# The FFN up projection: fourteen of 22 pairs take their seven products in a row, with other buffers

## The chip, the cores and the metric

The kernel runs on one core of a Trainium2 chip. Its engines have queues of their own: TensorE (PE; its weight loads are PEld), VectorE (DVE), ScalarE (ACT), GpSimd (POOL) and SyncE (SP), which issues every DMA here. Each queue runs in order, and engines wait for each other by semaphores. The metric is the time of one execution in microseconds (us) on the device; lower is better.

## The reference

One decoder layer on 1024 positions of 1024 channels in float32: a convolution branch and a state-space branch are mixed, then comes a ConvFFN. Only the ConvFFN's first half is touched:

```python
def conv_ffn(h, w_up, dw_w, dw_b, w_down):
    u = causal_dwconv(h @ w_up, dw_w, dw_b)        # w_up: 1024 x 5632, three taps
    gate, val = jnp.split(u, 2, axis=-1)           # 2816 channels each
    return (jax.nn.silu(gate) * val) @ w_down
```

## The kernel before

A float32 product is made of three matmuls of a rounded type: each operand is split into a high part (a ScalarE copy with rounding) and a low part (a VectorE subtraction), and `mm3` (lines 162 to 167) adds high x high, high x low and low x high into one bank. All matmuls of the ConvFFN thus carry lines 165 to 167, and all weight splits lines 153/154 (`weights`) or 730/731 (`split_pair`).

The up projection `h @ w_up` multiplies by Winograd's variant of Strassen's scheme: seven block products where eight would stand. A *pair* is one 128-channel block of the gate and one of the values. 22 pairs (`NF`) are made. The activations' blocks `b11`, `b21`, `b22` and sums `t1` to `t4` are prepared by `ffn_blocks`, which also holds the layer norm before it. A `product` (line 715) is four steps in depth, 12 matmuls of 128x512, into one of eight banks: four of the tag `acc` (`bank(1)`), four of the tag `sm` (`bank(0)`).

For pair j two products need the raw weights alone. `up_first` (line 805) loads them into `st_ue`, splits them as `w_ue`, makes w11 x b11, copies the result out (`s`, line 811), adds w21 x b21 into the same bank, and copies again (`c`, line 815). Both results go to `first_scr` in DRAM. The other five are made by `up_rest` (line 837). Its `up_weights` (line 818) loads both raw tiles of the pair again (`ra`, `rb`), makes sums of their halves in place on VectorE (lines 828 to 831), and splits three tiles: `w_s24`, `w_s10` and `w_s3` (lines 730/731, all named `w_s` in the trace; the sum of w3 is `s3`, shown as `s`). `s` and half of `ug` come back from `first_scr` (lines 846, 847). Three `sm` banks take five products (t2; t1; t3; b22 on top of t1's bank; t4 on top of t3's), and five VectorE instructions (lines 853 to 861) add or subtract them into `s`, `ug` and `uv` (`fug`, `fuv` in the trace). The convolution then takes one ScalarE scaling and two VectorE taps for each of the two blocks (lines 867, 871), ScalarE's silu (881) and the gating (882). Every second pair adds four block sums (896 to 899) and stores results for the down projection.

Order: eight firsts (`LEAD`) run ahead, while `ffn_blocks` ends; the 14 others are spread over the 22 calls of `up_rest`. Instructions are placed by a scheduler that plays the program through with planned times and takes what is ready by priority; `tc.high_priority(offset=...)` pulls loads and splits ahead. Each queue's order is then fixed. A pool lends buffers by tag: `wst` has three raw buffers (`st`), `wsp` three of split weights (`w`), `up` three of raw pair weights (`raw`). A tile waits until the earlier tile in its buffer is released. Pools that follow each other share memory: `up` takes that of `trans` (used by `ffn_blocks`), and `down` that of `ffq`.

The down projection (line 903) begins with eight `rows` loads (line 920), which need the buffer of the blocks b11 and b21, and its steps load `dr` raw tiles (952, 954), `c` tiles (955, 959) and split them (990, 991, `w_dn`). The tiles `c4` lie where `ffq` held b22, t1 and t2.

Of the kernel before, what the change touches and what calls it, by code (L numbers as in the profile page):

```python
# [21 lines left out]
FF = 2816  # L22
NF = FF // P
KC = 31
HEADS = 32
GROUPS = 4
HP = 64
# [28 lines left out]
def kernel(  # L56
# [30 lines left out]
    def bank(which):  # L87
        n_ps[0] += 1
        pl, tag = (pacc, "acc") if which else (psm, "sm")
        return pl.tile([P, 512], F32, tag=tag, name=f"{tag}{n_ps[0]}")  # L90
# [44 lines left out]

    h_scr = [dram.tile([HALF, D], F32, name=f"h_scr{i}") for i in range(2)]
    h1_scr = dram.tile([T, D], F32, name="h1_scr")
    first_scr = [dram.tile([2, P, HALF], F32, name=f"first_scr{j}") for j in range(NF)]
    NK = NF // 2
    b11_scr = [dram.tile([P, HALF], F32, name=f"b11_scr{k}") for k in range(NK)]  # L140
    b2_scr, t32_scr, t41_scr = (
# [660 lines left out]
            "t4": lambda i: b2[0][:, i, 4:8, :],  # L802
        }

    def up_first(qp, bl, j):

        w = weights(wup[2 * j], f"ue{j}")
        ps = bank(1)
        product(ps, lambda i: w[:, i, 0:HALF], bl["b11"], True)
        s1 = qp.tile([P, HALF], F32, tag="first", bufs=2, name=f"s1_{j}")  # L810
        A.copy(s1, ps)  # L811
        SY.dma_start(first_scr[j][0], s1)
        product(ps, lambda i: w[:, i, HALF:D], bl["b21"], False)
        c11 = qp.tile([P, HALF], F32, tag="first", bufs=2, name=f"c11_{j}")
        A.copy(c11, ps)
        SY.dma_start(first_scr[j][1], c11)

    def up_weights(upp, j):


        with tc.high_priority(offset=2000):
            r1 = upp.tile([P, D], F32, tag="raw", bufs=3, name=f"ra{j}")
            SY.dma_start(r1, wup[2 * j])
            r2 = upp.tile([P, D], F32, tag="raw", bufs=3, name=f"rb{j}")
            SY.dma_start(r2, wup[2 * j + 1])
            a11, a12, a21, a22 = r1[:, :HALF], r1[:, HALF:], r2[:, :HALF], r2[:, HALF:]
            s3 = upp.tile([P, HALF], F32, tag="s3", name=f"s3_{j}")
            V.tensor_tensor(out=s3, in0=a11, in1=a21, op=ALU.add)
            V.tensor_tensor(out=a21, in0=a21, in1=a22, op=ALU.add)
            V.tensor_tensor(out=a11, in0=a21, in1=a11, op=ALU.add)  # L830
            V.tensor_tensor(out=a12, in0=a12, in1=a11, op=ALU.add)
            w24 = split_pair(wsp, r1, f"s24_{j}")
            w10 = split_pair(wsp, r2, f"s10_{j}")
            w3 = split_pair(upp, s3, f"s3_{j}", HALF, 2)
        return w24, w10, w3

    def up_rest(upp, bl, j, before):

        w24, w10, w3 = up_weights(upp, j)
        ug, uv = (
            upp.tile([P, T + 32], F32, tag="u", bufs=3, name=f"f{n}{j}") for n in ("ug", "uv")
        )
        s = upp.tile([P, HALF], F32, tag="s", bufs=2, name=f"s{j}")
        SY.dma_start(s, first_scr[j][0])
        SY.dma_start(ug[:, 2 : 2 + HALF], first_scr[j][1])
        G.memset(ug[:, :2], 0.0)
        G.memset(uv[:, :2], 0.0)
        pb, pc_, pd = bank(0), bank(0), bank(0)  # L850
        late = slice(2 + HALF, 2 + T)
        product(pb, lambda i: w24[:, i, :HALF], bl["t2"], True)
        V.tensor_tensor(out=s, in0=s, in1=pb, op=ALU.add)
        product(pd, lambda i: w10[:, i, :HALF], bl["t1"], True)
        V.tensor_tensor(out=uv[:, late], in0=s, in1=pd, op=ALU.add)  # L855
        product(pc_, lambda i: w3[:, i], bl["t3"], True)
        V.tensor_tensor(out=uv[:, late], in0=pc_, in1=uv[:, late], op=ALU.subtract)
        product(pd, lambda i: w24[:, i, HALF:], bl["b22"], False)
        V.tensor_tensor(out=ug[:, late], in0=s, in1=pd, op=ALU.add)
        product(pc_, lambda i: w10[:, i, HALF:], bl["t4"], False)  # L860
        V.tensor_tensor(out=uv[:, 2 : 2 + HALF], in0=pc_, in1=s, op=ALU.subtract)
        os = []
        j = j // 2 + j % 2 * NK
        for jj, u in ((j, ug), (NF + j, uv)):
            o = upp.tile([P, T], F32, tag="o", bufs=3, name=f"fo{jj}")
            wc = PC_FW + 3 * jj
            A.activation(
                out=o, in_=u[:, 2 : 2 + T], func=AF.Identity, scale=pc[:, wc + 2 : wc + 3]
            )
            for k in range(2):  # L870
                V.scalar_tensor_tensor(  # L871
                    out=o,
                    in0=u[:, k : k + T],
                    scalar=pc[:, wc + k : wc + k + 1],
                    in1=o,
                    op0=ALU.mult,
                    op1=ALU.add,
                )
            os.append(o)
        og, ov = os  # L880
        A.activation(out=og, in_=og, func=AF.Silu, bias=pc[:, PC_FB + j : PC_FB + j + 1])
        V.scalar_tensor_tensor(
            out=ov,
            in0=ov,
            scalar=pc[:, PC_FB + NF + j : PC_FB + NF + j + 1],
            in1=og,
            op0=ALU.add,
            op1=ALU.mult,
        )
        early, late = slice(0, HALF), slice(HALF, T)  # L890
        if j < NK:
            SY.dma_start(b11_scr[j], ov[:, early])
            return ov
        SY.dma_start(b2_scr[j - NK], ov)
        a, b, t = before, ov, og
        V.tensor_tensor(out=t[:, early], in0=a[:, late], in1=b[:, late], op=ALU.subtract)
        V.tensor_tensor(out=a[:, late], in0=a[:, early], in1=a[:, late], op=ALU.subtract)
        V.tensor_tensor(out=t[:, late], in0=t[:, early], in1=a[:, early], op=ALU.subtract)
        V.tensor_tensor(out=a[:, early], in0=b[:, early], in1=t[:, late], op=ALU.add)
        SY.dma_start(t32_scr[j - NK], t)  # L900
        SY.dma_start(t41_scr[j - NK], a)

    def down(upp, dp, g, b):
# [32 lines left out]
        def load(p, k):  # L936
# [12 lines left out]
            with tc.high_priority(offset=4000):  # L949
                st = raw("dr")  # L950
                w_st = st[:, E]
                SY.dma_start(st[:, L], x)
                if p == 0:
                    SY.dma_start(w_st, a11)
                    SY.dma_start(c3[k], a21)
                    add(c3[k], c3[k], w_st)
                elif p == 1:
                    SY.dma_start(w_st, a12)
                    SY.dma_start(c4[k], a22)
                    add(c4[k], c4[k], w_st)  # L960
                elif p == 2:
                    SY.dma_start(w_st, a22)
                    add(w_st, w_st, c3[k])
                elif p == 3:
                    w_st = c3[k]
                    add(c4[k], c4[k], c3[k])
                elif p == 4:
                    other = raw("do")[:, E]
                    SY.dma_start(w_st, a21)
                    SY.dma_start(other, a22)  # L970
                    add(w_st, w_st, other)
                elif p == 5:
                    SY.dma_start(w_st, a22)
                else:
                    w_st = c4[k]
                if p == 6 and k >= NK - 4:
                    if not last:
                        last.append(big_tile("last").rearrange("p i k t -> p (i k t)"))
                    w = last[0][:, (k - NK + 4) * 2 * D : (k - NK + 5) * 2 * D]
                    w = w.rearrange("p (i n) -> p i n", i=2)  # L980
                else:
                    own = n_steps % 2 and n_steps > 4
                    w = (dp if own else wsp).tile(
                        [P, 2, D], F32R, tag="w", bufs=3, name=f"w_dn{p}_{k}"
                    )
                cuts = ((slice(0, D), st),) if w_st is not c3[k] and w_st is not c4[k] else (
                    (E, w_st), (L, st[:, L])
                )
                for cs, src in cuts:
                    A.copy(w[:, 0, cs], src)  # L990
                    V.tensor_tensor(  # L991
                        out=w[:, 1, cs], in0=src, in1=w[:, 0, cs].bitcast(F32), op=ALU.subtract
                    )
# [89 lines left out]
    qp = ffn_stack.enter_context(pool("ffq", side="right"))  # L1083
    with pool("trans") as tp:
        bl = ffn_blocks(tp, qp, mixT)
    n_first = 0

    def firsts_to(n):
        nonlocal n_first
        while n_first < min(n, NF):  # L1090
            up_first(qp, bl, n_first)
            n_first += 1

    LEAD = 8
    firsts_to(LEAD)
    upp = ctx.enter_context(pool("up"))
    before = None
    for j in range(NF):
        firsts_to(LEAD + (j + 1) * (NF - LEAD) // (NF - 1))
        before = up_rest(upp, bl, j, before)  # L1100
    ffn_stack.close()
    dp = ctx.enter_context(pool("down", side="right"))
# [101 lines left out]
```

## Time and profile before

| | us |
|---|---|
| median of three runs | 2030.39 (2029.87 to 2030.8) |
| profiled execution, its own time | 2030.96 |
| span of that execution | 2029.3 |
| first and last start of a `w_ue` matmul | 1356.0, 1767.4 |

The profile is of one execution. Times in rows are microseconds from the span's start, or of one instruction; names in a row are output <- inputs, without buffer numbers, so `acc<-h1b,w_ue` is a first product, `sm<-h1s,w_s` and `sm<-h1b,w_s` are the products of `up_rest`, and `acc<-w_dn` belongs to the down projection. A bracket behind a row gives how long the engine sat idle before it and what ended that. `SPq` rows are DMA issues. A matmul's duration overlaps the next one's; the distance of starts is the rate.

### The profile page before, as it was taken

To read this page: it belongs to the slowest core of one execution; us is meant where nothing else is said; L and a number is where in the kernel's file an instruction comes from. 1 tells how busy PE (TensorE), PEld (TensorE's weight loads), DVE (VectorE), ACT (ScalarE), POOL (GpSimd) and SP (SyncE) were. 2 spreads that over 40 slices of the span, in tenths; PEclk is the share of its full clock that TensorE was granted. 3 is DMA by queue.
4 is the path that set the end of the run, shared out by engine and by line. 5 is a ranking of instruction groups with operands and counts; after the bars stand their busy time and mean duration, and the time that the engine had idled before them with its cause. 6 is when DMAs were issued, how large, how long until landed. Compare 5 with 4: busy or idle time off the path is not lost. (4 is left out here: it accounts for less than half of the span.)

```text
span 2029.3 us, 24897 instructions
## 1 busy us (share of the span) xinstructions
PE 1973.4 (97%) x9164; PEld 1624.7 (80%) x9164; DVE 1732.8 (85%) x2307; ACT 987.5 (49%) x1403; POOL 147.1 (7%) x125
## 2 busy tenths in 40 slices
PE   7999999999999999999999999999999999989998
PEld 6888887888788888888888888887878788768886
DVE  7599999989766868999998976586899899889768
ACT  4465654556453265665454635364444344334432
POOL 2010101001400000100100121001000000000000
PEclk9999999999999999999999999999999999999999
DMA  6222233332545532222323254576545545578463
GB/s 219 94 64 93 80 102 106 98 105 99 166 126 194 214 104 73 89 83 84 115 89 117 96 171 129 169 252 223 166 161 199 169 161 197 184 292 279 161 226 109
DMA packets 109274, 297.14 MB, mean 146 GB/s; under 512 B 12384, under 2 KB 12384, under 8 KB 109152
## 3 DMA queue, kind: packets, MB, share of 16 engines
q1 hardware_dynamic: 109152, 295.55, 43.7%
q8 instruction: 72, 1.18, 0.2%
q14 instruction: 50, 0.41, 0.1%
HBM read 238.61 MB, written 56.89 MB: 146 GB/s over the span
## 5 line engine op out<-in xcount | busy, mean ns | idle before, releaser
L419 DVE SCALAR_TENSOR_TENSOR c<-v,pc,c 128x512 f32<-128x512 f32 x480 | 374.9, 804 | 8.4 <-ACT c L408 7.0
L477 POOL TENSOR_TENSOR au<-seg_mv,head_of 128x1024 fp32r<-128x1024 f32 x32 | 76.9, 2403 | 963.6 <-PE sm L486 730.1
L165 PE MATMUL acc<-hT,w_c 128*128 128x512 f32 x352 | 141.0, 401 | 0.0
L166 PE MATMUL acc<-hT,w_c 128*128 128x512 f32 x352 | 140.5, 399 | 0.0
L167 PE MATMUL acc<-hT,w_c 128*128 128x512 f32 x352 | 138.4, 393 | 0.0
L165 PE MATMUL sm<-h1s,w_s 128*128 128x512 f32 x264 | 104.6, 396 | 11.2 <-DVE fuv L855 9.1
L374 DVE SCALAR_TENSOR_TENSOR xbc<-u,pc,xbc 128x512 f32<-128x512 f32 x144 | 109.8, 775 | 0.7 <-ACT xbc L372 0.5
L990 ACT CAST w_dn<-dr 128x1024 fp32r<-128x1024 f32 (+1 forms) x73 | 68.7, 945 | 83.7 <-DVE dr L924 32.4
L166 PE MATMUL sm<-h1s,w_s 128*128 128x512 f32 x264 | 103.5, 392 | 0.0
L167 PE MATMUL sm<-h1s,w_s 128*128 128x512 f32 x264 | 102.8, 392 | 0.0
L166 PE MATMUL acc<-w_z,hT 128*128 128x512 f32 x256 | 100.8, 394 | 0.0
L165 PE MATMUL acc<-w_z,hT 128*128 128x512 f32 x256 | 100.8, 401 | 0.0
L167 PE MATMUL acc<-w_z,hT 128*128 128x512 f32 x256 | 100.7, 396 | 0.0
L153 ACT CAST w_c<-st_c 128x1024 fp32r<-128x1024 f32 x50 | 52.5, 1051 | 86.4 <-PE acc L167 65.6
L991 DVE TENSOR_TENSOR w_dn<-dr,w_dn 128x1024 fp32r<-128x1024 f32 (+1 forms) x73 | 78.9, 1089 | 11.2 <-ACT w_dn L990 11.1
L166 PEld LDWEIGHTS acc<-hT,w_c 128*128 128x128 f32 x352 | 66.1, 188 | 16.9 <-issue 3.8
L167 PEld LDWEIGHTS acc<-hT,w_c 128*128 128x128 f32 x352 | 66.1, 188 | 16.1 <-issue 2.6
L165 PEld LDWEIGHTS acc<-hT,w_c 128*128 128x128 f32 x352 | 66.1, 188 | 15.9 <-issue 2.6
L154 DVE TENSOR_TENSOR w_c<-st_c,w_c 128x1024 fp32r<-128x1024 f32 x47 | 60.6, 1289 | 20.3 <-ACT w_c L153 20.3
L165 PE MATMUL acc<-h1b,w_ue 128*128 128x512 f32 x176 | 70.0, 398 | 6.8 <-ACT s L811 6.8
L165 PEld LDWEIGHTS sm<-h1s,w_s 128*128 128x128 f32 x264 | 50.1, 190 | 25.9 <-DVE fuv L855 12.2
L166 PE MATMUL acc<-h1b,w_ue 128*128 128x512 f32 x176 | 69.5, 395 | 0.0
(336 smaller groups left out, 5723.1 us busy)
## 6 DMA issues: line engine op xcount, KB each, us to landing
st_c<-wcol SPq DMA_DIRECT2D x50, 512.0 KB, 3.6
st_z<-wz SPq DMA_DIRECT2D x32, 512.0 KB, 3.5
dr<-wdown SPq DMA_DIRECT2D x55, 256.0 KB, 4.5
st_wo<-wo SPq DMA_DIRECT2D x24, 512.0 KB, 4.0
st_ue<-wup SPq DMA_DIRECT2D x22, 512.0 KB, 3.8
ra<-wup SPq DMA_DIRECT2D x22, 512.0 KB, 3.6
rb<-wup SPq DMA_DIRECT2D x22, 512.0 KB, 3.9
t_scr<-fo SPq DMA_DIRECT2D x22, 512.0 KB, 3.5
```

The source lines that it names most:

```text
L153: A.copy(w[:, 0, :], st)
L154: (eng or V).tensor_tensor(out=w[:, 1, :], in0=st, in1=w[:, 0, :].bitcast(F32), op=ALU.subtract)
L165: TE.matmul(ps, wa(0), xa(0), start=start, stop=False, skip_group_check=more)
L166: TE.matmul(ps, wa(0), xa(1), start=False, stop=False, skip_group_check=more)
L167: TE.matmul(ps, wa(1), xa(0), start=False, stop=stop, skip_group_check=more)
L374: V.scalar_tensor_tensor(out=o, in0=u[:, k : k + HALF], scalar=pc[:, wc + k : wc + k + 1], in1=o, op0=ALU.mult, op1=ALU.add,)
L419: V.scalar_tensor_tensor(out=accs[i], in0=v[:, k : k + HALF], scalar=pc[:, wc + k : wc + k + 1], in1=accs[i], op0=ALU.mult, op1=ALU.add,)
L477: G.tensor_tensor(out=au, in0=seg_mv[:, c, :].unsqueeze(1).to_broadcast([P, 8, P]), in1=head_of[:, g, :].unsqueeze(2).to_broadcast([P, 8, P]),
L990: A.copy(w[:, 0, cs], src)
L991: V.tensor_tensor(out=w[:, 1, cs], in0=src, in1=w[:, 0, cs].bitcast(F32), op=ALU.subtract)
```

## The change

The firsts of pairs 0 to 7 run ahead as before, with a pool of their own (`firsts`, four buffers), which is closed before the pool `up` is opened. The 14 other pairs have no first any more: their seven products are made by `up_rest`, from one load of each raw tile. A third split, `w_ue`, is taken from `ra` before the sums overwrite it, in the pool `wsp`. Two `acc` banks are used (`ps`, `py`): b11, t2, t1 and b22 accumulate in `ps`, and ScalarE copies the bank out after each of them into `s`, `s`, `uv` and `ug`; b21 goes to `py`, which VectorE adds to `s`. VectorE thus has three evictions in such a pair in place of five. In all pairs t3 now comes before t1, and t4 before b22.

The raw tile `ra` moves to the pool `wst` (three buffers), and `rb` has the three of `up` to itself. In the down projection the split tiles use the pool `dp` from step 3 on, in place of step 5.

```diff
-    def up_first(qp, bl, j):
+    def up_first(fp, bl, j):
...
-        product(ps, lambda i: w[:, i, 0:HALF], bl["b11"], True)
-        s1 = qp.tile([P, HALF], F32, tag="first", bufs=2, name=f"s1_{j}")
-        A.copy(s1, ps)
-        SY.dma_start(first_scr[j][0], s1)
-        product(ps, lambda i: w[:, i, HALF:D], bl["b21"], False)
-        c11 = qp.tile([P, HALF], F32, tag="first", bufs=2, name=f"c11_{j}")
-        A.copy(c11, ps)
-        SY.dma_start(first_scr[j][1], c11)
+        for q, block in enumerate(("b11", "b21")):
+            product(ps, lambda i: w[:, i, q * HALF : (q + 1) * HALF], bl[block], q == 0)
+            f = fp.tile([P, HALF], F32, tag="first", bufs=4, name=f"first{q}_{j}")
+            A.copy(f, ps)
+            SY.dma_start(first_scr[j][q], f)
...
-            r1 = upp.tile([P, D], F32, tag="raw", bufs=3, name=f"ra{j}")
+            r1 = wst.tile([P, D], F32, tag="st", name=f"ra{j}")
...
+            ue = None if j < LEAD else split_pair(wsp, r1, f"ue{j}")
...
-        SY.dma_start(s, first_scr[j][0])
-        SY.dma_start(ug[:, 2 : 2 + HALF], first_scr[j][1])
...
-        pb, pc_, pd = bank(0), bank(0), bank(0)
-        late = slice(2 + HALF, 2 + T)
-        product(pb, lambda i: w24[:, i, :HALF], bl["t2"], True)
-        V.tensor_tensor(out=s, in0=s, in1=pb, op=ALU.add)
-        product(pd, lambda i: w10[:, i, :HALF], bl["t1"], True)
-        V.tensor_tensor(out=uv[:, late], in0=s, in1=pd, op=ALU.add)
-        product(pc_, lambda i: w3[:, i], bl["t3"], True)
-        V.tensor_tensor(out=uv[:, late], in0=pc_, in1=uv[:, late], op=ALU.subtract)
-        product(pd, lambda i: w24[:, i, HALF:], bl["b22"], False)
-        V.tensor_tensor(out=ug[:, late], in0=s, in1=pd, op=ALU.add)
-        product(pc_, lambda i: w10[:, i, HALF:], bl["t4"], False)
-        V.tensor_tensor(out=uv[:, 2 : 2 + HALF], in0=pc_, in1=s, op=ALU.subtract)
+        early, late = slice(2, 2 + HALF), slice(2 + HALF, 2 + T)
+        ps, pz = bank(1 if ue else 0), bank(0)
+        if ue:
+            product(ps, lambda i: ue[:, i, :HALF], bl["b11"], True)
+            A.copy(s, ps)
+            py = bank(1)
+            product(py, lambda i: ue[:, i, HALF:], bl["b21"], True)
+            V.tensor_tensor(out=ug[:, early], in0=s, in1=py, op=ALU.add)
+            product(ps, lambda i: w24[:, i, :HALF], bl["t2"], False)
+            A.copy(s, ps)
+        else:
+            SY.dma_start(s, first_scr[j][0])
+            SY.dma_start(ug[:, early], first_scr[j][1])
+            pu = bank(0)
+            product(pu, lambda i: w24[:, i, :HALF], bl["t2"], True)
+            V.tensor_tensor(out=s, in0=s, in1=pu, op=ALU.add)
+        product(pz, lambda i: w3[:, i], bl["t3"], True)
+        product(ps, lambda i: w10[:, i, :HALF], bl["t1"], not ue)
+        if ue:
+            A.copy(uv[:, late], ps)
+        else:
+            V.tensor_tensor(out=uv[:, late], in0=s, in1=ps, op=ALU.add)
+        V.tensor_tensor(out=uv[:, late], in0=pz, in1=uv[:, late], op=ALU.subtract)
+        product(pz, lambda i: w10[:, i, HALF:], bl["t4"], False)
+        V.tensor_tensor(out=uv[:, early], in0=pz, in1=s, op=ALU.subtract)
+        product(ps, lambda i: w24[:, i, HALF:], bl["b22"], False)
+        if ue:
+            A.copy(ug[:, late], ps)
+        else:
+            V.tensor_tensor(out=ug[:, late], in0=s, in1=ps, op=ALU.add)
...
-                    own = n_steps % 2 and n_steps > 4
+                    own = n_steps % 2 and n_steps > 2
...
-    firsts_to(LEAD)
+    with pool("firsts", side="right") as fp:
+        for j in range(LEAD):
+            up_first(fp, bl, j)
     upp = ctx.enter_context(pool("up"))
     before = None
     for j in range(NF):
-        firsts_to(LEAD + (j + 1) * (NF - LEAD) // (NF - 1))
         before = up_rest(upp, bl, j, before)
```

More of the change, by code (lines that the diff above doesn't have):

```diff
@@ L24 @@
 KC = 31
+LEAD = 8
 HEADS = 32
@@ L137 @@
     h1_scr = dram.tile([T, D], F32, name="h1_scr")
-    first_scr = [dram.tile([2, P, HALF], F32, name=f"first_scr{j}") for j in range(NF)]
+    first_scr = [dram.tile([2, P, HALF], F32, name=f"first_scr{j}") for j in range(LEAD)]
     NK = NF // 2
@@ L834, in up_weights @@
             w3 = split_pair(upp, s3, f"s3_{j}", HALF, 2)
-        return w24, w10, w3
+        return ue, w24, w10, w3
     def up_rest(upp, bl, j, before):
-        w24, w10, w3 = up_weights(upp, j)
+        ue, w24, w10, w3 = up_weights(upp, j)
         ug, uv = (
@@ L1085 @@
         bl = ffn_blocks(tp, qp, mixT)
[L1086 to L1094, printed above, removed]
-    firsts_to(LEAD)
+    with pool("firsts", side="right") as fp:
+        for j in range(LEAD):
+            up_first(fp, bl, j)
     upp = ctx.enter_context(pool("up"))
```

## The prediction

> **What bounds the kernel now.** I read the page first, then the stretches of the ConvFFN, then who TensorE waited for in them.
>
> ```profile
> span 2029.3 us, 24897 instructions
> PE 1973.4 (97%) x9164; PEld 1624.7 (80%) x9164; DVE 1732.8 (85%) x2307; ACT 987.5 (49%) x1403; POOL 147.1 (7%) x125
> ```
>
> TensorE is the bound, at 97% of the span, and the change leaves its matmuls alone, so only its lost time can change. The three stretches below are the lead of eight pairs, the 22 pairs, and the start of the down projection; columns: length, busy us (instructions) of PE, PEld, DVE, ACT, POOL, granted clock, DMA share, GB/s.
>
> ```profile
> 1356.00:1409.00 53.00, 48.26 (x210) 39.35 (x209) 41.35 (x57) 28.02 (x46) 7.83 (x8) 0.94 0.68 233
> 1409.00:1795.00 386.00, 372.57 (x1619) 303.67 (x1618) 342.48 (x409) 157.55 (x170) 3.97 (x40) 1.00 0.55 184
> 1795.00:1840.00 45.00, 40.53 (x172) 32.66 (x171) 38.16 (x45) 16.94 (x16) 0.10 (x1) 0.96 0.81 294
> ```
> ```profile
> 1398.30 0.39 PE L166 MATMUL acc<-h1b,w_ue 128*128 128x512 f32 x1
> 1398.53 0.39 PE L167 MATMUL acc<-h1b,w_ue 128*128 128x512 f32 x1
> 1403.66 0.80 PE L165 MATMUL acc<-h1b,w_ue 128*128 128x512 f32 x1 [4.74 <-ACT s L811]
> ...
> 1408.52 0.63 PE L167 MATMUL acc<-h1b,w_ue 128*128 128x512 f32 x1
> 1408.95 0.44 PE L165 MATMUL sm<-h1s,w_s 128*128 128x512 f32 x1
> ```
> ```profile
> PE sm L165 <- DVE fuv L855: 9.1, 6, 2.7
> PE acc L165 <- ACT s L811: 6.8, 4, 4.7
> PE sm L165 <- ACT w_s L730: 2.1, 3, 1.1
> ```
> ```profile
> PE acc L165 <- ACT w_dn L990: 4.5, 1, 4.5
> ```
>
> Matmuls follow each other every 0.2267 us (1398.30 to 1398.53), so one product (12) takes 2.72 us. Room in the 22 pairs: 386 - 1619 x 0.2267 = 19.0 us. Of that, 13.3 are waits (9.1 for VectorE's eviction, 6.8 - 4.7 for the first copy, 2.1 for splits). Ahead of them the end of the lead loses 4.9 us in one wait and 2.4 more because the 12 matmuls behind it follow at 0.43; the down projection starts with a wait of 4.5.
>
> VectorE is nearly a second bound, 342.5 of 386 us. Its back-to-back prices are the distances of starts:
>
> ```profile
> 1450.08 0.69 DVE L829 TENSOR_TENSOR rb<-rb 128x512 f32<-128x512 f32 x1
> 1450.68 0.68 DVE L853 TENSOR_TENSOR s<-s,sm 128x512 f32<-128x512 f32 x1
> ...
> 1451.88 1.28 DVE L871 SCALAR_TENSOR_TENSOR fo<-fuv,pc,fo 128x1024 f32<-128x1024 f32 x1
> 1453.07 0.68 DVE L830 TENSOR_TENSOR ra<-rb,ra 128x512 f32<-128x512 f32 x1
> ...
> 1457.28 1.21 DVE L731 TENSOR_TENSOR w_s<-ra,w_s 128x1024 fp32r<-128x1024 f32 x1
> 1458.41 0.68 DVE L897 TENSOR_TENSOR fo<-fo 128x512 f32<-128x512 f32 x1
> ```
>
> That is 0.60 for 512 columns, 1.13 for a 1024-column split, 1.20 for a tap of the convolution. One pair costs VectorE 4 sums (2.4), splits of w24, w10 and w3 (2.86), 5 evictions (3.0), 4 taps and the gating (6.0) and half of four block sums (1.2): 15.46 us. The ue split adds 1.13.
>
> **The change, part by part.** *Removed work.* 14 loads of `st_ue`, 28 stores and 28 loads of `first_scr` leave SP's queue (70 issues, 14 x 0.5 + 56 x 0.25 = 21 MB), and 28 evictions leave VectorE (28 x 0.60 = 16.8 us); 28 copies join ScalarE, 28 x 0.587 = 16.4 us by the row below, beside 157.6 busy of 386. None of it is on TensorE's path by itself: DMA was at 0.55. I cost the ScalarE copies at nothing, since two to five microseconds of other products stand between a copy and the matmul that reuses its bank in the new order of TensorE; without that cover each would cost about 0.6.
>
> ```profile
> L811 ACT COPY s<-acc 128x512 f32<-128x512 f32 x22 | 12.9, 587 | 71.4 <-PE acc L167 48.4 <-issue 23.0
> L828 DVE TENSOR_TENSOR s<-ra,rb 128x512 f32<-128x512 f32 x21 | 14.5, 690 | 13.9 <-DMA rb<-wup 12.8 <-DMA t_scr<-fo 1.0
> ```
>
> *Raw tiles in two rings.* VectorE waited 12.8 us for `rb`, because ra and rb shared three buffers. With three each that wait goes. It helps only where VectorE is the late one.
>
> *The 22 pairs are now two regimes.* Before, the 14 later firsts were spread over the 22 pairs. Now pairs 0 to 7 have five products each and no filler: TensorE 5 x 2.72 = 13.6 us, VectorE 15.46. Pairs 8 to 21 have seven: TensorE 19.04, VectorE 15.46 + 1.13 - 2 x 0.60 = 15.4. So VectorE is short by 1.86 us in each of the first eight, and has 3.6 to spare in the rest. In the program's order of TensorE four products of pairs 8 and 9 (w3 and both ue of 8, w3 of 9) stand ahead of pair 7's last two, which covers the end; the shortage shows over the five pairs 1 to 5: about 5 x 1.86 = 9.3 us, with pair 0 free because VectorE starts ahead of TensorE. Its bounds are 0 (all absorbed) and 8 x 1.86 = 14.9. In the rest VectorE's 9.1 go; the copy and split waits, 2.1 + 2.1 over 22 pairs, stay for 14: 2.7, and about 2 of the 5.7 that are no wait. Sum 9.3 + 4.7 = 14.0 against 19.0: **-5.0**, bounds -14 (the shortage absorbed) and +10 (below).
>
> [...]
>
> *Start of the pairs.* The weights of pair 0 need `rb0`.
>
> ```profile
> 1392.53 0.38 SPq L825 DMA_DIRECT2D rb<-wup  x1
> ...
> 1403.02 0.32 SPq L816 DMA_DIRECT2D first_scr<-c  x1
> ```
> ```profile
> DMA to landing us min/median/max: 3.4/3.9/8.8
> ```
> ```profile
> 1400.42 0.69 DVE L828 TENSOR_TENSOR s<-ra,rb 128x512 f32<-128x512 f32 x1 [6.87 <-DMA rb<-wup]
> ```
> ```profile
> 1403.86 1.04 ACT L730 CAST w_s<-ra 128x1024 fp32r<-128x1024 f32 x1 [0.25 <-DVE ra L831]
> ```
>
> Before, SP issued it at 1392.5, while TensorE still had firsts, though ScalarE's split for it stood ahead of two copies and made the 4.7 us wait. In the changed program the ScalarE copies come first, so TensorE runs through: its last matmul of the lead starts at 1398.53 + 12 x 0.2267 = 1401.25. But SP's queue now has rb0 (then rb1, rb2 and the loads of s and fug) behind the store of the very last copy. That copy (0.59) ends about 1402.4, the store takes 0.32, rb0 is issued about 1402.8 and lands 3.9 later (the rows of all rb), 1406.7. From landing (1400.4) to the end of the w24 cast (1404.9) it took 4.5 before; one sum of pair 1 now stands in it: 5.1. TensorE restarts about 1411.8, idle for 10.3, then 2.4 at half rate: 12.7 against 4.9 + 2.4. **+5.4**, bounds +4.9 and +10.3 (landing 3.4 to 8.8).
>
> [...]
>
> ```profile
> 1617.01 0.61 PE L165 MATMUL sm<-h1s,w_s 128*128 128x512 f32 x1 [2.69 <-DVE fuv L855]
> 1617.42 0.63 PE L166 MATMUL sm<-h1s,w_s 128*128 128x512 f32 x1
> ```
>
> *Into the down projection.* `own` from step 3 moves one split tile, hidden. SP decides:
>
> ```profile
> 1768.32 1.79 SPq L920 DMA_DIRECT2D rows<-h_scr  x4
> ...
> 1803.88 2.70 SPq L959 DMA_DIRECT2D c<-wdown  x6
> 1806.68 7.85 SPq L955 DMA_DIRECT2D c<-wdown  x11
> 1814.88 1.68 SPq L959 DMA_DIRECT2D c<-wdown  x3
> 1817.28 0.33 SPq L952 DMA_DIRECT2D dr<-b_scr  x1
> 1817.66 0.42 SPq L954 DMA_DIRECT2D dr<-wdown  x1
> ```
> ```profile
> 1823.52 1.04 ACT L990 CAST w_dn<-dr 128x1024 fp32r<-128x1024 f32 x1 [10.87 <-DMA dr<-wdown]
> ```
>
> The loads of c (256 KB, 7.85 / 11 = 0.71 us each) wait for the last pair's products; the seventh raw tile stands behind them and ends the 4.5 us wait. In the changed order one more c load, a b11 store and the two 512 KB rows of ln2 stand ahead of it: four issues of 0.56 (1.68 / 3) or six units of 0.71, +2.2 to +4.3, less 0.7 for three more matmuls of cover. Besides, `rows` waits for the end of ue 21, 35.6 us ahead of the c loads before (1768.3 to 1803.9), 69 matmuls = 15.6 us ahead after; 26 units of 256 KB stand between, 18.5 us, so up to 2.9 more. **+5.0**, bounds +1.5 and +6.5; I take 5 because both rows point to a full queue.
>
> Sum: -5.0 + 5.4 + 5.0 = +5.4 on the profiled execution's own 2030.96, which is 0.57 above the median of three runs; so 2036.4 less 0.57: about **2036 us** against 2030.4. 0.2% is 4 us, about what a measurement tells from no change.
>
> **The rivals.**
> - *No overlap*: the shortage of all eight pairs shows, 14.9 instead of 9.3: 2041. For it: every split of the next pair is VectorE work too. Against: the order does pull products ahead.
> - *The shortage is absorbed*, for which VectorE must enter pair 0 some 9 us ahead and stay ahead: 2036 - 9.3 = 2026.5, not slower. For it: the 12.8 us of waits for rb are gone. Against: VectorE's last eviction of pair 0 must wait for pair 0's last product, which uses up a head start. It decides if the shortage is under 4 us.
> - *The split ring*: three buffers hold ue, w24 and w10 of one pair, so each of 14 pairs has three casts that can start only when TensorE releases a buffer. At the longest split wait of before, 1.1 us for each pair, 15.4 instead of 4.7: 2047. Against: by the order 2.7 us of another product stand behind each release, and cast and split take 1.04 + 1.13.
> - *The down projection's wait does not grow*: 2031, no difference.
>
> **How the numbers follow.** Forecast 0.36, no overlap 0.14, ring 0.18, down wait unchanged 0.16, absorbed 0.16. The range leaves out little: from 2027 (absorbed) to 2047 (ring). Slower by over 0.2% (above 2034.5) holds most of the forecast, no overlap and the ring: 0.6; within: the unchanged wait and half of the absorbed: 0.26; faster: the rest, 0.14. The forecast's own range is 2032 to 2040.
>
> **What would show it.** Right: a TensorE wait of 10 us or so at about 1401, ended by a ScalarE split behind `rb`; VectorE without gaps up to about 1530, with TensorE waits for `fuv` there of some 9 us in all, and VectorE idle beyond it; the wait for `w_dn` at some 9 us. Wrong: rb0 landing before the last first; waits for ScalarE copies or `w_s` splits in pairs 8 to 21 over 5 us; a `w_dn` wait of 5 or less.

## The result, and the profile after

The changed kernel takes 2043.26 us (median, 2041.94 to 2046.89) against 2030.13: ratio 1.0067, 95% interval 1.0054 to 1.008, so about 13 us slower. The profiled execution took 2044.79 us by its own time, 13.8 more than that of before. The forecast was 2036 (range 2027 to 2047).

The head of the page, then the table by stage (same columns as in the prediction): start, eight lead pairs, 14 full pairs, start of the down projection.

```profile
span 2043.0 us, 24683 instructions
...
PE 1977.0 (97%) x9164; PEld 1627.7 (80%) x9164; DVE 1717.1 (84%) x2279; ACT 1001.3 (49%) x1431; POOL 146.8 (7%) x125
```
```profile
1356.00:1417.00 61.00, 49.81 (x218) 40.51 (x218) 44.48 (x63) 30.16 (x49) 7.54 (x8) 0.92 0.55 202
1417.00:1545.00 128.00, 115.08 (x478) 92.78 (x478) 110.94 (x137) 44.48 (x45) 1.31 (x13) 0.95 0.38 131
1545.00:1812.00 267.00, 264.54 (x1164) 217.54 (x1163) 216.13 (x244) 124.44 (x150) 2.82 (x28) 1.00 0.32 115
1812.00:1850.00 38.00, 31.11 (x123) 24.52 (x122) 34.18 (x38) 16.33 (x17) 0.00 (x0) 0.91 1.04 384
```

Time lost is length less matmuls x 0.2267, as in the prediction:

| stretch | before | after | difference |
|---|---|---|---|
| start of the pairs | 5.4 | 11.6 | +6.2 |
| 22 pairs | 19.0 | 19.6 + 3.1 | +3.7 |
| start of the down projection | 6.0 | 10.1 | +4.1 |

The sum, +14.0, agrees with the measured 13.8. TensorE's waits (engine, tile, line, who ended them; us in total, times, longest), in the order of the stretches:

```profile
PE sm L166 <- ACT w_s L731: 10.0, 1, 10.0
PE acc L166 <- ACT first L814: 1.2, 1, 1.2
...
PE sm L166 <- DVE fuv L869: 12.3, 3, 5.2
...
PE acc L166 <- ACT w_ue L731: 1.4, 1, 1.4
PE acc L166 <- ACT fuv L867: 1.1, 2, 0.8
...
PE acc L166 <- ACT w_dn L1006: 4.4, 1, 4.4
PE acc L167 <- DVE w_dn L1007: 2.5, 2, 1.3
```

The lead pairs are the surprise: 12.3 us of waits for VectorE, and more behind them. Two of the three waits for `fuv` are followed by matmuls at half rate, 0.43 us from start to start, one by matmuls at the usual 0.23 (TensorE's timeline; start, duration):

```profile
1445.82 0.50 PE L166 MATMUL sm<-h1s,w_s 128*128 128x512 f32 x1 [2.67 <-DVE fuv L869]
1446.16 0.40 PE L167 MATMUL sm<-h1s,w_s 128*128 128x512 f32 x1
...
1478.79 0.80 PE L166 MATMUL sm<-h1s,w_s 128*128 128x512 f32 x1 [5.17 <-DVE fuv L869]
...
1484.51 0.61 PE L167 MATMUL sm<-h1b,w_s 128*128 128x512 f32 x1
...
1513.70 0.79 PE L166 MATMUL sm<-h1s,w_s 128*128 128x512 f32 x1 [4.50 <-DVE fuv L869]
...
1518.56 0.63 PE L168 MATMUL sm<-h1s,w_s 128*128 128x512 f32 x1
```

From 1478.79 to 1484.51 TensorE starts 14 matmuls, 13 steps that take 5.7 us where 2.9 would do; from 1513.70 to 1518.56 it takes 11 steps in 4.9 us where 2.5 would do. That is some 5 us. And VectorE, 110.94 busy of 128, was not without gaps there. What it waited for, 1417 to 1545:

```profile
DVE fug L877 <- PE sm L168: 5.2, 2, 2.6
DVE w_s L732 <- ACT w_s L731: 3.9, 4, 2.7
DVE fuv L872 <- PE sm L168: 2.7, 1, 2.7
```

TensorE waits for VectorE (L869), and VectorE then waits for TensorE (L877): b22 is added to the bank that L869 has to read first, and L877 adds that bank to `s` when b22 is in. The wait of L872 (2.7) lies in pair 0, ahead of all this. ScalarE's splits held VectorE for 3.9 more. L877 behind the first and the second of the three waits above:

```profile
1449.29 0.67 DVE L877 TENSOR_TENSOR fug<-s,sm 128x512 f32<-128x512 f32 x1
...
1484.32 0.69 DVE L877 TENSOR_TENSOR fug<-s,sm 128x512 f32<-128x512 f32 x1 [2.59 <-PE sm L168]
```

The first, where b22 ran at the usual rate, didn't make VectorE wait; the second and the third, at half rate, cost it 2.59 each, the 5.2 of the table. At the usual rate of 0.2267 the twelve matmuls of b22 from 1478.79 would have ended near 1481.7, when VectorE ended the gating before L877. So, by this estimate, the half rate costs twice here: TensorE's own time, and VectorE's wait for its result.

### The profile page after: what moved, and what is told of

It reads as the page before. It is cut to its first block, busy times and chain, and to the rows that moved or that the text cites. A ratio compares the mean times of both kernels' runs of the same rounds, so it can differ in the third digit from the quotient of the medians.

```text
span 2043.0 us, 24683 instructions
## 1 busy us (share of the span) xinstructions
PE 1977.0 (97%) x9164; PEld 1627.7 (80%) x9164; DVE 1717.1 (84%) x2279; ACT 1001.3 (49%) x1431; POOL 146.8 (7%) x125
## 5 line engine op out<-in xcount | busy, mean ns | idle before, releaser
L731 ACT CAST w_s<-rb 128x1024 fp32r<-128x1024 f32 x22 | 23.2, 1053 | 94.7 <-PE sm L168 73.1
L166 PE MATMUL sm<-h1b,w_s 128*128 128x512 f32 x176 | 69.4, 395 | 0.0
L167 PE MATMUL sm<-h1b,w_s 128*128 128x512 f32 x176 | 69.2, 393 | 0.0
L168 PE MATMUL sm<-h1b,w_s 128*128 128x512 f32 x176 | 69.0, 392 | 0.0
```

Of the source, the lines that this page charges most:

```text
L166: TE.matmul(ps, wa(0), xa(0), start=start, stop=False, skip_group_check=more)
L167: TE.matmul(ps, wa(0), xa(1), start=False, stop=False, skip_group_check=more)
L168: TE.matmul(ps, wa(1), xa(0), start=False, stop=stop, skip_group_check=more)
L731: A.copy(w[:, 0, :], src)
```

## The experiments

Times are medians; the kernel before, timed beside them, stayed between 2029.6 and 2030.2. "After" is the changed kernel, 2043.26.

**The same lead pairs, spread.**

```diff
-LEAD = 8
+LEAD = tuple(range(0, NF, 3))
...
-            ue = None if j < LEAD else split_pair(wsp, r1, f"ue{j}")
+            ue = None if j in LEAD else split_pair(wsp, r1, f"ue{j}")
...
```

> The changed kernel with the same eight run-ahead pairs, but as pairs 0, 3, 6, 9, 12, 15, 18 and 21 instead of 0 to 7; the work is the same, only the order of lead and full pairs differs. Theory (two regimes: VectorE is short by 1.86 us in a lead pair and has 3.6 us to spare in a full one, and the changed kernel puts all the short ones in a row): the TensorE waits for fuv and the half rate behind them (19.6 us lost in the eight lead pairs) mostly go, a lead pair's shortage being made up in the two full ones behind it; 14 to 17 us less than the changed kernel, so 2026 to 2030 us and about the time of the kernel before. Rival one (the lead pairs lose their time to the raw ring and to ScalarE's splits, wherever they stand): the 2.5 us per lead pair stay, 2040 to 2046 us. Rival two (VectorE has no slack between full pairs, because its work there waits for ScalarE's copies): new waits in the full pairs, less than 8 us gained.

2029.69 us, ratio to the kernel before 1.0 (0.999 to 1.0009): 13.6 us less than after. The stretch of all 22 pairs, TensorE's waits in it, and the matmul behind its wait for `w_dn`:

```profile
1416.00:1795.00 379.00, 375.70 (x1646) 307.34 (x1645) 327.85 (x383) 174.05 (x197) 4.11 (x41) 1.00 0.38 131
```
```profile
PE acc L166 <- ACT fuv L867: 2.6, 7, 0.8
PE sm L166 <- DVE fuv L869: 0.7, 1, 0.7
```
```profile
1820.37 1.22 PE L166 MATMUL acc<-w_dn 128*128 128x512 f32 x2 [7.79 <-ACT w_dn L1006]
```

379 - 1646 x 0.2267 = 5.9 lost, where the changed kernel loses 22.7. The work is the same and only its order differs, so it is the eight in a row that cost. A lead pair as the last one lengthens the wait for `w_dn` to 7.79.

**A lighter VectorE in the lead pairs.**

```diff
-            for k in range(2):
+            for k in range(2 if ue else 1):
```

> The changed kernel with one of the two VectorE taps of each of both convolutions left out in pairs 0 to 7, so that part of the depthwise convolution is not computed there; it takes 2 x 1.20 = 2.4 us of VectorE off each lead pair (15.46 to 13.06 us, under TensorE's 13.6) and no other engine's work. Theory (VectorE's load sets the lead pairs' length): the waits for fuv at about 1446, 1479 and 1514 us go with their half rate, 128 us of the eight lead pairs become 112 to 115; 12 to 16 us less, 2027 to 2031 us. Rival (the lead pairs go by a ping-pong of TensorE, VectorE and ScalarE with only two buffers each, in which VectorE is idle 17 us of 128): less than 7 us gained, and VectorE's idle time in that stretch grows by about as much as its work shrinks.

2035.23 us, 8.0 less than after: between the two expectations. Lead pairs, full pairs, and the waits in each:

```profile
1417.00:1528.00 111.00, 109.30 (x476) 88.70 (x476) 97.37 (x126) 44.86 (x46) 1.40 (x14) 1.00 0.45 155
1528.00:1795.00 267.00, 259.70 (x1137) 212.21 (x1136) 204.64 (x234) 120.01 (x146) 2.58 (x26) 1.00 0.30 107
```
```profile
PE sm L168 <- DVE w_s L732: 1.1, 3, 0.4
...
PE acc L166 <- ACT w_ue L731: 7.0, 5, 1.4
```

All waits for `fuv` are gone and the lead pairs lose 3.1 instead of 19.6, a little more than the gain that the theory gives; so without VectorE's load the loss doesn't arise. But the full pairs now lose 9.2 (267 - 1137 x 0.2267) instead of 3.1: TensorE waits 1.4 us for a split of `w_ue` five times. Before the first of these waits ScalarE's queue stood:

```profile
1600.06 1.05 ACT L731 CAST w_s<-rb 128x1024 fp32r<-128x1024 f32 x1 [9.56 <-PE sm L168]
1601.01 1.04 ACT L731 CAST w_ue<-ra 128x1024 fp32r<-128x1024 f32 x1
```

The cast of w10 waits until TensorE releases a buffer, and the cast of `w_ue` stands behind it. That is the prediction's rival of the split ring; 6 of 16 us are given back to it. The changed kernel has one such wait, and the kernel with the lead pairs spread has none, so a VectorE that isn't late doesn't bring them by itself; what does stays open.

**Twelve in a row.**

```diff
-LEAD = 8
+LEAD = 12
```

> The changed kernel with twelve pairs run ahead in a row instead of eight. Theory as measured (once VectorE is late, each lead pair in a row costs TensorE 2.5 to 3.3 us: VectorE's shortage, the half rate behind each wait, and VectorE's own wait for TensorE after it): 4 x 2.5 to 4 x 3.3, so 10 to 13 us slower than the changed kernel, 2053 to 2056 us. By the shortage of 1.86 us alone: 7.4 us slower, 2051 us. Rival (the eight lead pairs lose at their start only, while the load of the weights catches up): within 3 us of the changed kernel.

2054.68 us, ratio 1.0129 (1.0113 to 1.0144), 11.4 more than after, 2.9 for each further lead pair in a row and not 1.86. In the stretch of its lead pairs 195 - 717 x 0.2267 = 32.5 us are lost:

```profile
1445.00:1640.00 195.00, 173.94 (x717) 139.36 (x716) 172.43 (x209) 69.97 (x70) 2.20 (x22) 0.95 0.39 132
```

**The pool of the pairs opened first.**

```diff
+    upp = ctx.enter_context(pool("up"))
     with pool("firsts", side="right") as fp:
...
-    upp = ctx.enter_context(pool("up"))
...
-            f = fp.tile([P, HALF], F32, tag="first", bufs=4, name=f"first{q}_{j}")
+            f = fp.tile([P, HALF], F32, tag="first", bufs=2, name=f"first{q}_{j}")
```

> The changed kernel with the tile pool of the pairs (up) opened ahead of that of the run-ahead results, which keeps two buffers instead of four, so that the load of rb0 needn't wait for the store of the last run-ahead result. Theory (the start of the pairs is late because rb0 stands in SP's queue behind that store): rb0 is loaded some 8 us earlier, the TensorE wait of 9.99 us for the first split of w_s shrinks to 2 to 5 us and its half rate with it; 4 to 8 us less, 2035 to 2039 us. Rival (the first split waits for the additions on VectorE and the split on ScalarE, not for the load): the wait stays within 1.5 us of 9.99, and the time within 2 us of the changed kernel's. Second rival: with two buffers the run-ahead products wait for their stores (2 us each), which gives back what the early load gains.

2036.47 us, 6.8 less than after. SP's queue of after, then of this kernel, and this one's first product of pair 0:

```profile
1394.40 9.52 SPq L815 DMA_DIRECT2D first_scr<-first  x5
1403.97 1.39 SPq L824 DMA_DIRECT2D rb<-wup  x3
```
```profile
1394.95 3.23 SPq L824 DMA_DIRECT2D rb<-wup  x3
```
```profile
1406.78 0.80 PE L166 MATMUL sm<-h1s,w_s 128*128 128x512 f32 x1 [4.89 <-ACT w_s L731]
```

The loads of `rb` leave 9 us earlier, the wait of 9.99 is 4.89 and that of 1.2 for the copy of a first is gone: rb0 behind the last store was the cause of the late start. In the lead pairs TensorE's waits for `fuv` stay (12.4 us, 12.3 before the edit), so the start isn't what makes them.

**The rows of the down projection later.**

```diff
...
-        for t in range(8):
-            SY.dma_start(rs[t], h1_scr[t * P : (t + 1) * P, :])
...
+                if p == 0 and k == NK - 3:
+                    for t in range(8):
+                        SY.dma_start(rs[t], h1_scr[t * P : (t + 1) * P, :])
+                if p == 1 and k == 4:
+                    g, b = row(dp, RW_2G, D, "ln2_g"), row(dp, RW_2B, D, "ln2_b")
...
```

> The changed kernel with the loads of the down projection's residual rows (eight of h1) and of the two rows of the last layer norm issued inside the first products of the down projection instead of ahead of them. Theory (the first weights of the down projection come late because 4 MB of rows stand ahead of them in SP's queue): the three waits for w_dn (1.2, 1.3 and 4.4 us) and the half rate behind them shrink, 2 to 6 us less, 2037 to 2041 us. Rival (the first weights wait for their raw buffers, which the last pair's splits free, or for the transfer of its own outputs): the time stays within 1.5 us of the changed kernel's. Second rival: the rows come too late for the layer norm or collide with the weights of the second product, up to 5 us slower.

2044.89 us, 1.6 more than after: in amount the second rival, in place none of the three. The waits for `w_dn` at the start of the down projection went, as the theory has it, but a new one of 6.2 us stands in the last pair (SP, ScalarE, TensorE's waits):

```profile
1800.43 3.40 SPq L970 DMA_DIRECT2D c<-wdown  x4
1804.17 0.33 SPq L910 DMA_DIRECT2D b_scr<-fo  x1
```
```profile
1810.57 1.15 ACT L883 ACTIVATE fo<-fug,pc 128x1024 f32<-128x1024 f32 x1 [5.80 <-DMA b_scr<-fo]
```
```profile
PE acc L166 <- ACT fuv L867: 6.5, 2, 6.2
```

Loads of `c` took the place of the rows ahead of a store of a pair's output, which SP issued at 1797.51 in the changed kernel and at 1804.17 here; ScalarE waits for that output's buffer, with the last pair's copy behind it in its queue (at 1815.50), and TensorE waits for the copy. The gain went into a new wait, because what was moved out of SP's queue let other loads move up past a store.

**`own` undone.**

```diff
-                    own = n_steps % 2 and n_steps > 2
+                    own = n_steps % 2 and n_steps > 4
```

> The changed kernel with the condition in the down projection's loads back at the value it has before the change (a step's split tiles come from their own pool from the fifth odd step on, not from the third). Theory (the first waits for w_dn come from VectorE's lateness and from the loads, not from the ring of split tiles): within 1.5 us of the changed kernel, 2042 to 2045 us. Rival (at the third step the ring is still held by the last pair's split tiles): a wait for w_dn of 2 us or more in addition to the 4.38 us, 2045 to 2048 us.

2044.39 us (2042.55 to 2046.72), 1.1 more than after, inside its spread: hidden, as the prediction had it.

**The copies on VectorE.** All four of a full pair:

```diff
-            A.copy(s, ps)
+            V.tensor_copy(s, ps)
```

> The changed kernel with the four copies of a full pair out of the two banks done by VectorE instead of ScalarE (14 pairs, four copies of 128x512 each). Theory (VectorE has 15.4 us of work in a full pair of 19.04 us, so four copies more, 2.4 us, still fit; only the lag carried over from the lead pairs is made up later): 0 to 5 us slower than the changed kernel, 2043 to 2048 us. Rival (the copies on ScalarE were what makes the full pairs fast; on VectorE each stands behind taps and splits and TensorE waits for its bank): over 14 us slower, 1 us or more in each full pair, 2057 us or more.

2049.95 us, 6.7 more than after, a little over the theory's 5 and far from the rival's 14. In the full pairs 267 - 1156 x 0.2267 = 4.9 are lost where it was 3.1, with VectorE at 242.5 of 267; the rest is spread over the other stretches. The copies were worth moving to ScalarE, but they aren't what makes the full pairs run without gaps.

```profile
1547.00:1814.00 267.00, 264.31 (x1156) 215.90 (x1154) 242.52 (x296) 95.32 (x94) 2.70 (x27) 1.00 0.32 112
```

**The raw rings, undone in the changed kernel and alone in the kernel before.**

```diff
-            r1 = wst.tile([P, D], F32, tag="st", name=f"ra{j}")
+            r1 = upp.tile([P, D], F32, tag="raw", bufs=3, name=f"ra{j}")
```

> The changed kernel with the ring of raw tiles undone: ra comes from the pairs' own ring again, three buffers for ra and rb together, instead of from the weights' ring. Theory (the rings matter little: in the lead pairs VectorE's work is the limit, in the full pairs 6.8 us a pair are free on the queue's side): 0 to 4 us slower than the changed kernel, 2043 to 2047 us, from waits of VectorE's first addition for rb. Rival (three buffers for two loads per pair bind in the full pairs, where a pair takes 19 us and its ra is held until its last split): 1 us or more in each of 14 pairs, 2057 us or more. If the time falls, the two rings cost something at the start, and that is where it would show.

The opposite edit in the kernel before:

> The kernel before with the ring of raw tiles alone changed: ra comes from the weights' ring, rb from the pairs' own. Theory (in the kernel before VectorE waits 12.8 us in all for rb in its first addition, idle that mostly lies beside TensorE's work): within 3 us of the kernel before, 2027 to 2032 us. Rival one (the loads set the pace of the pairs there): 5 us or more faster, 2025 us or less. Rival two (the weights' ring is still held by the run-ahead products, so that ra0 comes later): the start of the pairs is 2 to 6 us later, 2032 to 2036 us.

Both theories fell, in opposite directions. Alone, two rings take the kernel before to 2020.85 us (ratio 0.9957, 0.9942 to 0.9972), 9.3 less, where the first rival had put it. Undone in the changed kernel, the time falls too: 2036.28 us, 7.0 less than after. The 22 pairs of the first:

```profile
1408.00:1789.00 381.00, 377.49 (x1654) 310.83 (x1653) 344.17 (x411) 158.29 (x170) 4.08 (x41) 1.00 0.56 189
```

It loses 6.0 there, not 19.0; its VectorE waits for `rb` no more. For the second, the stretch from VectorE's first sum of pair 0 to its eighth gating is to be compared; first of after, then with one ring, with VectorE's waits for TensorE there:

```profile
1407.89:1563.70 155.81, 137.88 (x569) 111.60 (x570) 137.19 (x169) 57.30 (x59) 1.61 (x16) 0.93 0.37 130
```
```profile
DVE fug L877 <- PE sm L168: 6.3, 3, 2.6
...
DVE fuv L872 <- PE sm L168: 2.7, 1, 2.7
```
```profile
1411.02:1558.10 147.08, 134.51 (x557) 107.87 (x558) 133.67 (x162) 56.92 (x59) 1.59 (x16) 0.94 0.41 141
```
```profile
DVE fuv L872 <- PE sm L168: 1.7, 1, 1.7
...
DVE fug L877 <- PE sm L168: 0.8, 2, 0.5
```

With one ring it is 8.7 us shorter: 3.5 less of VectorE's work, since fewer later weights are prepared in it, and 5.2 less idle; its waits for TensorE are 2.5 instead of 9.0. That the work done ahead is the cause was tried:

```diff
-            r2 = upp.tile([P, D], F32, tag="raw", bufs=3, name=f"rb{j}")
+            r2 = upp.tile([P, D], F32, tag="raw", bufs=2, name=f"rb{j}")
...
-            return pl.tile([P, D], F32, tag=tag, bufs=3, name=f"{name}_{n_raw}")
+            return pl.tile([P, D], F32, tag=tag, bufs=3 if pl is wst else 2, name=f"{name}_{n_raw}")
```

> The changed kernel with ra in the weights' ring as there, but two buffers instead of three for rb (and for the down projection's raw tiles of that ring). VectorE's order then has the weight sums of three pairs begun ahead of the first eviction and of nine ahead of pair 7's, against four and ten in the changed kernel and two and nine in the kernel with ra and rb in one ring, which lost 13.9 us in the lead pairs where the changed kernel lost 19.6. Theory (working one pair further ahead on weights, 4 x 0.60 + 2.86 = 5.3 us of VectorE, is what the lead pairs pay for while VectorE is the limit): 13 to 16 us lost in the lead pairs. Rival (ra in the weights' ring costs by itself, by its loads or the start): 18 to 21 us lost there. The down projection, which loses a raw buffer too, may lose some 1 to 4 us more at its start or along it; so the time is 2037 to 2043 us by the theory, 2043 to 2048 us by the rival.

2050.5 us (2048.12 to 2060.45), and in the lead pairs 124 - 432 x 0.2267 = 26.1 lost. No run meets the theory's 2037 to 2043 us, and none the rival's 2043 to 2048, though the fastest (2048.12) all but does. But the profiled execution was the slowest, 10 us above the median, so its 26.1 is no measure of the others; and the edit also takes a buffer from the down projection, whose wait for `w_dn` is 10.3 here. So neither is shown: the theory isn't borne out, and the rival isn't excluded.

```profile
1425.00:1549.00 124.00, 104.15 (x432) 83.82 (x431) 102.69 (x124) 43.39 (x43) 1.20 (x12) 0.93 0.37 125
```
```profile
DVE fug L877 <- PE sm L168: 7.0, 3, 3.3
DVE fuv L872 <- PE sm L168: 6.1, 1, 6.1
```

Again VectorE waits for TensorE, 13.1 here. Over the stretch from the first sum to the eighth gating TensorE loses 20.8 us with one ring, 26.8 in the changed kernel and 31.8 in this execution (165.56 - 590 x 0.2267), where VectorE's waits for it are 2.5, 9.0 and 14.5: the loss goes with these waits in all three. Why two rings bring more of them stays open.

**Spread, with full pairs at both ends.**

```diff
-LEAD = tuple(range(0, NF, 3))
+LEAD = (1, 4, 6, 9, 11, 14, 16, 19)
```

> The changed kernel with the eight run-ahead pairs as pairs 1, 4, 6, 9, 11, 14, 16 and 19: spread, and neither the first pair nor the last two among them. With the lead pairs at 0, 3, ..., 21 the time was 2029.7 us, with a wait of 10.84 us at the start of the pairs (rb0) and one of 7.79 us for w_dn behind the last lead pair. Theory (a full pair's first two products use ra alone, so 5.4 us of rb0's lateness lie beside them; a lead pair at the end leaves VectorE late for the down projection's splits): the start wait shrinks to 3 to 6 us, the wait for w_dn to 2 to 5 us; 6 to 13 us less than with 0, 3, ..., 21, so 2017 to 2024 us, under the kernel before. Rival one (the first full pair's split of w_ue and its copies come as late as rb0 did): the start wait stays within 2 us of 10.8, 2024 to 2029 us. Rival two (the waits for w_dn come from SP's queue, not from VectorE): the end stays as it is, 2023 to 2026 us.

2021.04 us, ratio 0.996 (0.9946 to 0.9974). The start's wait is 6.24 instead of 10.84, that for `w_dn` 2.78 instead of 7.79:

```profile
1414.68 0.79 PE L166 MATMUL sm<-h1b,w_s 128*128 128x512 f32 x1 [6.24 <-ACT w_s L731]
```

**The same with the pool opened first.**

Both edits shown above together, the new list of lead pairs and the pool.

> The kernel with lead pairs 1, 4, 6, 9, 11, 14, 16 and 19 and, with it, the pairs' pool opened ahead of that of the run-ahead results (two buffers for these). Theory (rb0's load behind the store of the last run-ahead result is all that is late at the start): the wait at the start goes nearly away, 2 to 5 us less than with the lead pairs alone. Rival (the full first pair hides rb0 already): within 1.5 us of the kernel with the lead pairs alone.

2013.0 us, ratio 0.9923 (0.9909 to 0.9938), the fastest kernel here; 8.0 less, more than expected. No wait at the start is left (379 - 1649 x 0.2267 = 5.2 us are lost from 1400 to the end of the pairs):

```profile
1400.00:1779.00 379.00, 376.81 (x1649) 308.21 (x1648) 328.64 (x388) 174.22 (x199) 4.00 (x40) 1.00 0.39 132
```

## Why the prediction was right, and where it wasn't

Sign and range held; the time was 7 us short, and nearly all of that is one term. 2043 lies above the forecast's own 2032 to 2040. It is inside the range because the split ring, which cost 1.4 us once, had been allowed up to 2047; that is luck.

- *Start of the pairs, +5.4*: +6.2. The mechanism was the one named: `rb0` issued at 1403.97 (forecast 1402.8), TensorE idle 9.99 (10.3). Opening the pool first gave 6.8 back. The extra 1.2 is a wait between the last two firsts for ScalarE's copy, which the prediction had at nothing.
- *The 22 pairs, -5.0*: +3.7, the term that failed. Its full pairs were right, 3.1 for 4.7, and so was VectorE's slack there. The step "the shortage shows over the five pairs 1 to 5: about 5 x 1.86 = 9.3" was mis-sized: 19.6. The cause stands, shown from both sides: VectorE made lighter, or the pairs spread, and the loss goes; four more in a row, and the time grows by 11.4. Three things were missing. First, the prediction has no term for half rate behind the waits of these eight pairs: 24 steps in 10.6 us where 5.4 would do, so some 5 us of TensorE's time. Second, "VectorE without gaps": it was idle 17 of 128 us, 8.5 of them waiting back for TensorE (5.2 behind half rate, 2.7 in pair 0 and two short ones). Its work in the stretch, 110.9, is only 2.6 more than TensorE's 478 x 0.2267 = 108.4; the other 17 of the 19.6 are this idle time. The shortage worked out from the two engines' sums was too low here, where each also waited for the other. Third, the two rings: the prediction gave them only the end of VectorE's waits for `rb`. They were worth 9.3 in the old order and cost 7.0 in the new one.
- *Into the down projection, +5.0*: +4.1, but not as told. The wait for ScalarE's `w_dn` stayed at 4.4 (forecast some 9), though the prediction had named 5 or less as a sign that it was wrong; most of the growth is two waits for VectorE's half of a split (2.5 in all), and behind the wait of 4.4 about twelve matmuls at half rate (0.43 to 0.47 us each) where it was seven. That 4.1 is near 5.0 is luck. With the rows out of SP's way a wait of 6.2 took the place of these, so what the rows were worth can't be read from it.
- *Copies at nothing, `own` hidden*: right; 1.1 us in all for copies in the full pairs, no difference for `own`.
- *Rivals.* "No overlap" (14.9 in the lead pairs, 2041) was nearest; spreading the pairs shows that the order is what costs, and 19.6 that even this rival was too cheap. "Absorbed" fell with the waits for `fuv`. The split ring cost 1.4 us once here, but five times when VectorE was lighter in the lead pairs: it is real, and its price depends on the order. "The wait for `w_dn` doesn't grow" is right to the letter, and the stretch grew all the same.

## What to carry to other kernels

When a change makes two kinds of work out of one, keep each engine's sum for each kind, and then ask whether the kinds alternate or come in a row: the same 22 pairs took 2043 us with the VectorE-heavy ones in a row and 2013 with them between the others, full pairs at both ends, and the loads not queued behind a store. Price a shortage above the difference of the sums when the short engine also waits for the other one (19.6 us lost here where the sums differ by 2.6), and look in the trace at the rate of the matmuls behind each wait as well as at its length (12 matmuls at 0.43 instead of 0.2267 cost 2.4 us here). A part that helps alone (two rings, -9.3) can hurt in another order (+7.0), so its worth has to be measured in the kernel that it goes into.

## What the runs showed of the hardware

Whether matmuls at half rate (0.43 us from start to start instead of 0.2267) follow a wait wasn't settled by its length between 2.3 and 3.1 us. Behind a wait of 2.73 in the fastest kernel the next starts 0.59 later and takes 0.63, like those at half rate; behind one of 3.08 in the kernel with late rows it starts 0.34 later and takes 0.40:

```profile
1782.80 0.80 PE L166 MATMUL acc<-h1s,w_s 128*128 128x512 f32 x1 [2.73 <-ACT fuv L867]
1783.39 0.63 PE L167 MATMUL acc<-h1s,w_s 128*128 128x512 f32 x1
```
```profile
1447.51 0.50 PE L166 MATMUL sm<-h1s,w_s 128*128 128x512 f32 x1 [3.08 <-DVE fuv L869]
1447.85 0.40 PE L167 MATMUL sm<-h1s,w_s 128*128 128x512 f32 x1
```

In the kernel before, a wait of 2.69 was followed by half rate (eight steps of 0.41 to 0.43), one of 2.37 was not (0.23); in the changed kernel one of 2.67 was not (0.23). All six waits of 4.38 us and more from the lead on in these two kernels were followed by it, and the longest wait didn't have the most of it (steps of 0.42 to 0.43 in a row):

| wait, us | kernel | steps |
|---|---|---|
| 4.38 | after | 8 |
| 4.45 | before | 5 |
| 4.50 | after | 11 |
| 4.74 | before | 11 |
| 5.17 | after | 13 |
| 9.99 | after | 7 |

It began behind the first matmul, or a few later: behind the wait of 4.45 the first four took 1.38, and then 0.59 and the five steps came.
